# A two-layer hybrid block on one core: attention's side projections in three-matmul steps

## The chip, the cores and the metric

The kernel runs on one core of a Trainium2 chip. A core has TensorE (PE: matmuls and weight loads), VectorE (DVE), ScalarE (ACT), GpSimd (POOL) and SyncE (SP), which here only issues DMAs. The metric is the device time of one execution in microseconds. Each engine works through its own instructions in a fixed order and waits on semaphores for the others.

## The reference

A block of depth 2 on 512 tokens of width 1024, all in float32. Each layer normalises the input, projects it by one wide matrix, runs three branches on the parts (attention, retention, a gated convolution of 31 taps), mixes them by gates and adds a feed-forward part:

```python
for l in range(DEPTH):
    h = _rmsnorm(x, norm_mix[l])
    z = h @ w_in[l]
    (q_n, kc, vc, ks, vs, kw, vw, g_n, q_r, k_r, v_r, g_r, c_a, c_b, m_g) = _split_cols(z)
    o_nsa = _nsa(q_n, kc, vc, ks, vs, kw, vw, g_n, ...)
    o_ret = _retention(q_r, k_r, v_r, g_r, ret_gn[l])
    o_conv = _conv_module(c_a, c_b, conv_w[l], ...)
    proj = jnp.einsum('bsnc,ncd->bsnd', br, w_branch[l])
    gate = jax.nn.sigmoid(m_g.astype(jnp.float32)).reshape(B, S, N_BRANCH, D_MODEL)
    merged = jnp.sum(gate * proj, axis=2).astype(x.dtype)
    x = x + merged @ w_out[l]
    h2 = _rmsnorm(x, norm_mlp[l])
    x = x + jnp.square(jax.nn.relu(h2 @ w_ff1[l])) @ w_ff2[l]
```

The attention has 8 heads in 2 groups. Each head attends to 31 compressed blocks, to selected blocks and to a window, with a bias by distance; three gates weigh the three results. With 512 tokens the selection takes every block, and the window reaches over all.

## The kernel before, in words

Activations lie transposed: channels on the partitions, 512 tokens along the free dimension. Every operand of a large matmul is split into a high and a low part, and `proj` adds up three matmuls for each of the 8 channel blocks (high by high, high by low, low by high): 24 matmuls of 512 columns for one 128-wide output, 12 where the input has 4 blocks. A weight block is loaded by SP into one of three `wr` buffers (L139), rounded by ScalarE into `wh` (L145), and its remainder is taken by GpSimd in two halves into `wl` (L148), three buffers each; in the feed-forward part VectorE takes the remainder (L150).

A layer runs in these stages. The norm. Retention over 4 heads, with the inputs of the convolution made between them; the convolution's 124 taps are VectorE instructions of 512 columns (L338), put in small numbers behind other VectorE instructions by `conv_taps_behind` (`T_ROT`, `T_SCORE`, `T_KEYS`). The keys: two compressions (`compress`), one set of side work (`F_KEYS`), two key projections (L556 to L563), the values for all 4 token blocks in 4 PSUM tiles (`mm` three times and `av`, L568 to L576), and 6 taps behind them. Attention: 4 pairs of heads, each pair one query projection (`query`, L643) and 4 blocks (2 heads by 2 branches). A block has 4 slots by token block: scores into `sc` (L707), bias and maximum on VectorE (L712), exponential on ScalarE (L714), the scale by gate and sum (`gate_over`, L627 to L629), and then for each slot a scaled copy (L719), 1 to 4 transposes into `tp` (L722), a rounded copy by ScalarE (L727) and the remainder by VectorE (L728); the block ends with 8 matmuls by the values into `av`. The rest of the taps is spread over the first 52 of 64 slots, then the convolution's norm runs in parts (`conv_norm`). Then the mix of the branches, the output projection and the feed-forward part.

Beside the attention runs side work, the list `pending`: 8 mixes of retention's result (a gate of 24 matmuls and a branch projection of 12) and 16 gates for the other branches, stored to DRAM until they are needed. One goes ahead of the keys. `fill` writes out whole units: 19 are dealt over the 16 blocks, each traced at the end of its block and allowed on TensorE once that block's first score was issued; 4 are kept for the end:

```python
u = 4 * j + k
with tc.issue_after(marks[u].ins):
    fill(paced * (u + 1) // 16 - paced * u // 16)
```

The order on each engine comes from a planner. It walks the program with times of its own, takes the ready instruction that was traced first, and so may put later instructions ahead of earlier ones that it holds to be waiting; `tc.issue_after(i)` adds that what is traced inside stands behind `i` on `i`'s engine. Tiles of one tag share `bufs` buffers, in SBUF pools that open and close by stage: the pool `att` of attention takes memory that `keys` gave back, and its tiles wait for the last use there. `bias` and `tq` lie in `att`. The bias tables are written to DRAM in the first layer's keys stage (`late_setup`, L264 to L266) and read by L661. PSUM has 3 buffers for `mm`, 2 for `sc`, 2 for `tp`, 1 for `av`.

Of the kernel before, what the change touches and what calls it, by code (L numbers as in the profile page):

```python
# [14 lines left out]
OP = mybir.AluOpType  # L15
AX = mybir.AxisListType

P = 128
# [3 lines left out]
KC = D // P  # L22
# [44 lines left out]
def block_kernel(ctx: ExitStack, tc: tile.TileContext, a, out):  # L67
# [9 lines left out]

    T_ROT, T_SCORE, T_KEYS, T_SLOTS = 1, 2, 3, 52


    AHEAD, F_KEYS, HELD = 16, 1, 4

# [74 lines left out]
    def proj(o, w, x, nk=KC):  # L157

        h, l = w
        for k in range(nk):  # L160
            xh, xl = x[k]
            mm(o, h[:, k, :], xh, k == 0, False)
            mm(o, h[:, k, :], xl, False, False)
            last = mm(o, l[:, k, :], xh, False, k == nk - 1)
        return last

# [103 lines left out]
    for l in range(DEPTH):  # L270
# [117 lines left out]
        for h in range(4):  # L388
# [45 lines left out]
            hh, ll = bo(), bo()  # L434
            split(hh, ll, ot)
            RO.append((hh, ll))
# [5 lines left out]
        gated = set()  # L442

        def gate(n, m):
            pg = ps("mm")
            proj(pg, wblock(w_f[FB_MG + n * KC + m]), X)
            t = tl(base, "g", 3)
            nc.vector.tensor_mul(t, pg, rs)
            nc.scalar.activation(t, t, AF.Tanh, scale=0.5)
            return t  # L450

        def gate_ahead(n, m):
            dma(gdram[n * KC + m], gate(n, m))
            gated.add((n, m))

        def mix(n, o, m):
            if (n, m) in gated:
                t = tl(base, "g", 3)
                dma(t, gdram[n * KC + m])
            else:  # L460
                t = gate(n, m)
            po = ps("mm")
            proj(po, wblock(a["w_b"][l, n, m], 4), o, 4)
            nc.vector.scalar_tensor_tensor(t, t, 1.0, po, op0=OP.add, op1=OP.mult)
            if n == 1:
                dma(mdram[m], t)
            else:
                nc.vector.tensor_add(merged[m], merged[m], t)

        pending = [lambda m=m: mix(1, RO, m) for m in range(KC)]  # L470
        pending += [lambda k=k: gate_ahead(2 * (k // KC), k % KC) for k in range(AHEAD)]
        paced = len(pending) - F_KEYS - HELD

        def fill(n):
            for _ in range(min(n, len(pending))):
                pending.pop(0)()

# [6 lines left out]

        def compress(fb, w1, w2, pe_at, is_k):
            pz = ps("mm")
# [28 lines left out]
            if is_k:  # L515
                hid = small((P, 62))
                nc.vector.scalar_tensor_tensor(hid, s, 1.0, ph[:, :62], op0=OP.add, op1=OP.mult)
                w2t = small((P, P))
                dma(w2t[:, 0:64], w2)
                dma(w2t[:, 64:128], w2)  # L520
# [12 lines left out]
            w2t = small((P, 64))  # L533
            dma(w2t, w2)
            pv = ps("tp")
# [10 lines left out]

        kcb = compress(FB_KC, a["cmp_w1_k"][l], a["cmp_w2_k"][l], 32, True)
        vcb = compress(FB_VC, a["cmp_w1_v"][l], a["cmp_w2_v"][l], 48, False)

        fill(F_KEYS)  # L550
        KHH, KLL = {}, {}
        for br, fb in ((0, FB_KS), (1, FB_KW)):
# [4 lines left out]
            for g in range(2):  # L557
# [4 lines left out]
                for half in (nat, oth):  # L562
                    low = nc.vector.tensor_sub(KLL[br, g][half], t[nat], f(KHH[br, g][nat]))  # L563
            conv_taps_behind(low, T_KEYS)
        G = tl(mix_pool, "G", 1, (P, NB, 24))
        V = []
        pz = [ps(tag) for tag in ("mm", "mm", "mm", "av")]
        proj_tok([p[:, :280] for p in pz], [(a["w_v"][l][:, k0:k0 + nk], nk) for k0, nk in ((0, 3), (3, 3), (6, 2))], 280, X)  # L568
        for i in range(NB):
# [6 lines left out]
            V.append(v)  # L576
        conv_taps_behind(low, 2 * T_KEYS)
        phase.close()
# [63 lines left out]

        def query(j):  # L643
            w = wblock(w_f[FB_Q + j])
            pq = ps("mm")
            proj(pq, w, X)
            tq = tl(ap, "tq", 2)
            nc.vector.scalar_tensor_tensor(tq, pq, -0.125, rs, op0=OP.mult, op1=OP.mult)
            return tq

        def attention_pair(j, tq, more):
            QS, bias = [], []
            for g in range(2):
                nat, oth = halves(g)
                q = tl(ap, "QS", 3, (P, T), FR)
                nc.scalar.activation(q[nat], tq[nat], AF.Copy)
                nc.vector.tensor_sub(q[oth], tq[nat], f(q[nat]))
                QS.append(q)
                t = tl(ap, "bias", 3)
                src = fd[g * HPG + j]  # L660
                dma(t, bass.AP(tensor=src.tensor, offset=src.offset + P - 1, ap=[[FLEN - 1, P], [1, T]]))  # L661
                bias.append(t)
# [32 lines left out]
            for g in range(2):  # L695
# [4 lines left out]
                for br in range(2):  # L700
# [3 lines left out]
                    for i in range(NB):  # L704
                        n = P * (i + 1)
                        sc = ps("sc")
                        m0 = mm(sc[:, :n], QS[g][:, i * P:(i + 1) * P], KHH[br, g][:, :n], True, False)  # L707
                        if i == 0:
                            marks.append(m0)
                        mm(sc[:, :n], QS[g][:, i * P:(i + 1) * P], KLL[br, g][:, :n], False, True)  # L710
# [3 lines left out]
                        nc.scalar.activation(s, s, AF.Exp, scale=-1.0, bias=mx[:, i:i + 1], accum_out=den[:, i:i + 1])  # L714
                        cols.append(s)
                    c = gate_over(den, h, 1 + br)
                    ph, pl = tl(ap, "pt", 4, (P, 1280), FR), tl(ap, "pt", 4, (P, 1280), FR)
                    for i in range(NB):
                        nc.scalar.activation(cols[i], cols[i], AF.Copy, scale=c[:, i:i + 1])  # L719
                        pt = ps("tp")  # L720
                        for k in range(i + 1):
                            nc.tensor.transpose(pt[:, k * P:(k + 1) * P], cols[i][:, k * P:(k + 1) * P], ident)  # L722
                        for (vh, ks), (vl, _) in zip(pt_views(ph, i), pt_views(pl, i)):
# [17 lines left out]

        ON, marks, tqs = [], [], [query(0)]
        late_taps = len(todo)

        def more(j, k):

            if k == 0 and j + 1 < HPG:
                tqs.append(query(j + 1))
# [139 lines left out]
```

## Time and profile before

| what | value |
|---|---|
| time, median of 3 runs | 1802.95 us (1802.86 to 1805.15) |
| the profiled execution, its own time | 1804.74 us |
| its span, first to last instruction | 1803.0 us |
| mean granted TensorE clock | 0.984 |
| TensorE busy | 1757.3 us, 97% |
| weight loads busy | 1473.8 us, 82% |
| VectorE busy | 1104.4 us, 61% |
| ScalarE busy | 774.9 us, 43% |
| GpSimd busy | 500.6 us, 28% |
| DMA, mean | 109 GB/s |

The span is the time from the first to the last instruction; the execution's own time has a little around it. A matmul's end is modelled and matmuls overlap, so a busy TensorE need not be at its peak; the granted clock says at what share of its full rate it was allowed to run. Weight loads run beside matmuls. Idle time of an engine that sets no end costs nothing.

### The profile page before, as it was taken

How to read it: one execution, taken by the hardware profiler on the slowest of the kernel's cores; microseconds unless marked ns; L12 is line 12 of the kernel's file. 1: busy time of each engine (PE TensorE's matmuls, PEld its weight loads, DVE VectorE, ACT ScalarE, POOL GpSimd, SP SyncE). 2: the span in 40 equal slices, each digit the busy share in tenths (PEclk: the TensorE clock that was granted, in tenths of full speed). 3: DMA queues.
4: the chain of work that ended last, by engine and by line, in shares of the span. 5: the costliest groups of instructions: out<-in, count | busy, mean ns of one | idle time of the engine just before them, and what ended most of it. 6: DMA issues, size and time to landing. Idle time of an engine off the chain costs nothing.

```text
span 1803.0 us, 23260 instructions
## 1 busy us (share of the span) xinstructions
PE 1757.3 (97%) x8592; PEld 1473.8 (82%) x8592; DVE 1104.4 (61%) x1979; ACT 774.9 (43%) x1421; POOL 500.6 (28%) x420
## 2 busy tenths in 40 slices
PE   8899899989999999999999999999899999999997
PEld 7788788868888888888898888888688888888886
DVE  6976978887554344434459778878857443434344
ACT  4433466766343232323434344667553341323241
POOL 4454444323471000000255543343137500000000
PEclk9999999989999999999999999999899999999998
DMA  4222623221753323333422232332147323332321
GB/s 167 87 88 61 203 94 122 96 71 65 233 169 96 101 96 93 95 96 102 135 94 89 87 127 83 98 131 90 41 161 227 119 94 94 93 94 94 105 85 68
DMA packets 70802, 195.82 MB, mean 109 GB/s; under 512 B 8945, under 2 KB 9329, under 8 KB 70689
## 3 DMA queue, kind: packets, MB, share of 16 engines
q1 hardware_dynamic: 70688, 194.34, 33.6%
q8 instruction: 68, 1.11, 0.3%
q14 instruction: 46, 0.37, 0.1%
HBM read 177.51 MB, written 19.42 MB: 109 GB/s over the span
## 4 chain that ended last, share of the span: by engine, by line
PE 67%; issue 20%; DVE 10%; ACT 2%; DMA 1%; SPq 0%; POOLq 0%; POOL 0%; DVEq 0%; ACTq 0%
PE mm L109 58%; PE sc L109 3%; DVE yc L338 3%; PE av L109 3%; PE tp L722 2%; PE tp L109 1%; DVE XP L500 1%; DVE kv L563 1%; DVE qk L386 1%; ACT s L719 0%; DVE pt L728 0%; ACT wh L145 0%; DVE rr L364 0%; PE tp L190 0%; DVE s L712 0%
## 5 line engine op out<-in xcount | busy, mean ns | idle before, releaser
L109 PE MATMUL mm<-X,wh 128*128 128x512 f32 x2432 | 777.4, 396 | 12.2 <-ACT X L214 6.1
L148 POOL TENSOR_TENSOR wl<-wr,wh 128x512 fp32r<-128x512 f32 (+2 forms) x344 | 436.2, 1290 | 563.2 <-ACT wh L145 540.6
L145 ACT ACTIVATE wh<-wr 128x1024 fp32r<-128x1024 f32 (+2 forms) x301 | 296.9, 987 | 681.9 <-PE mm L109 554.5
L109 PEld LDWEIGHTS mm<-X,wh 128*128 128x128 f32 x2432 | 455.3, 189 | 103.1 <-ACT X L214 6.3
L109 PE MATMUL mm<-X,wl 128*128 128x512 f32 x1216 | 479.5, 394 | 0.4 <-DVE wl L150 0.4
L109 PEld LDWEIGHTS mm<-X,wl 128*128 128x128 f32 x1216 | 230.2, 189 | 46.5 <-DVE wl L150 0.9
L338 DVE SCALAR_TENSOR_TENSOR yc<-u,ccol,yc 128x512 f32<-128x512 f32 x240 | 214.2, 894 | 1.7
L150 DVE TENSOR_TENSOR wl<-wr,wh 128x1024 fp32r<-128x1024 f32 x129 | 158.1, 1225 | 38.4 <-ACT wh L145 38.4
L109 PE MATMUL mm<-fa,wh 128*128 128x512 f32 x512 | 160.2, 395 | 0.0
L109 PE MATMUL mm<-bo,wh 128*128 128x512 f32 x512 | 160.0, 391 | 0.0
L805 DVE SCALAR_TENSOR_TENSOR t<-mm,rs 128x512 f32<-128x512 f32 x64 | 43.9, 691 | 161.5 <-PE mm L109 155.9
L227 POOL TENSOR_TENSOR t<-t,t 128x512 f32<-128x512 f32 x18 | 27.4, 1523 | 333.7 <-DVE wl L150 310.7
L206 POOL TENSOR_TENSOR n<-n,mhalf 128x4 f32<-128x4 f32 x15 | 16.5, 1101 | 372.3 <-DVE n L204 372.3
L109 PE MATMUL mm<-kv,wh 128*128 128x512 f32 x384 | 119.5, 389 | 0.0
L109 PEld LDWEIGHTS mm<-fa,wh 128*128 128x128 f32 x512 | 96.1, 188 | 23.2
L109 PEld LDWEIGHTS mm<-bo,wh 128*128 128x128 f32 x512 | 96.0, 188 | 19.7
L109 PE MATMUL mm<-fa,wl 128*128 128x512 f32 x256 | 100.5, 395 | 0.0
L109 PE MATMUL mm<-bo,wl 128*128 128x512 f32 x256 | 100.2, 392 | 0.0
L714 ACT ACTIVATE s<-s,n 128x128 f32<-128x128 f32 (+3 forms) x128 | 71.4, 559 | 46.9 <-DVE n L712 46.3
L109 PE MATMUL mm<-wh,X 128*128 128x256 f32 (+1 forms) x480 | 90.1, 286 | 0.0
L728 DVE TENSOR_TENSOR pt<-tp,pt 128x128 fp32r<-128x128 f32 (+1 forms) x192 | 70.0, 372 | 32.7 <-ACT pt L727 32.4
L816 DVE TENSOR_TENSOR yc<-yc,mm 128x512 f32<-128x512 f32 x32 | 22.0, 687 | 105.6 <-PE mm L109 105.6
(219 smaller groups left out, 2463.9 us busy)
## 6 DMA issues: line engine op xcount, KB each, us to landing
wr<-in_w_dram SPq DMA_DIRECT2D x128, 512.0 KB, 3.5
wr<-in_w_f_dram SPq DMA_DIRECT2D x87, 512.0 KB, 3.3
wr<-in_w_b_dram SPq DMA_DIRECT2D x48, 256.0 KB, 2.7
wr<-in_w_t_dram SPq DMA_DIRECT2D x16, 512.0 KB, 3.4
gd<-g SPq DMA_DIRECT2D x32, 256.0 KB, 2.0
g<-gd SPq DMA_DIRECT2D x32, 256.0 KB, 2.8
wr<-in_w_o_dram SPq DMA_DIRECT2D x16, 512.0 KB, 3.6
md<-g SPq DMA_DIRECT2D x16, 256.0 KB, 2.9
```

The lines of the kernel that those rows point to most:

```text
L109: return nc.tensor.matmul(o, l, r, start=start, stop=stop)
L145: nc.scalar.activation(h, t, AF.Copy)
L148: nc.gpsimd.tensor_sub(l[:, k], t[:, k], f(h[:, k]))
L150: nc.vector.tensor_sub(l, t, f(h))
L227: (nc.vector if c == KC - 1 or first_time else nc.gpsimd).tensor_add(s, s, acc)
L338: nc.vector.scalar_tensor_tensor(yc[c], x, w, yc[c], op0=OP.mult, op1=OP.add)
L386: nc.vector.tensor_sub(QLr[h][half], pt[nat], f(QHr[h][nat]))
L714: nc.scalar.activation(s, s, AF.Exp, scale=-1.0, bias=mx[:, i:i + 1], accum_out=den[:, i:i + 1])
L722: nc.tensor.transpose(pt[:, k * P:(k + 1) * P], cols[i][:, k * P:(k + 1) * P], ident)
L728: low = nc.vector.tensor_sub(vl, src, f(vh))
L805: nc.vector.scalar_tensor_tensor(t, pf, 0.0, rs, op0=OP.max, op1=OP.mult)
L816: nc.vector.tensor_add(xT[m], xT[m], pf)
```

## The change

The side work becomes generators. `proj_steps` yields after each three matmuls, and mixes and gates are written in such steps. A function `step(n)` runs the next n steps: 24 behind the first score of the first block, 5 behind the last score of each block of the last pair, and the rest, but for 16 that are left to the end, dealt evenly over the 64 slots, each behind the slot's last transpose. The weight block of a unit is asked for when its first step is taken. The bias tiles move to the layer's pool. The first query is projected ahead of the values, into a tile of the layer's pool. The second weights of the compressions are loaded at the start of the keys stage. The 6 taps behind the values are gone, 2 taps are added behind each retention head. `gate_ahead` is unpacked in the same way as the mix below; lines that only follow are left out.

```diff
-    T_ROT, T_SCORE, T_KEYS, T_SLOTS = 1, 2, 3, 52
-    AHEAD, F_KEYS, HELD = 16, 1, 4
+    T_ROT, T_SCORE, T_HEAD, T_KEYS, T_SLOTS = 1, 2, 2, 3, 52
+    AHEAD, F_KEYS, RAMP, HELD, LAST = 16, 1, 24, 5, 16
...
+    def proj_steps(o, w, x, nk=KC):
+
         h, l = w
         for k in range(nk):
             xh, xl = x[k]
             mm(o, h[:, k, :], xh, k == 0, False)
             mm(o, h[:, k, :], xl, False, False)
-            last = mm(o, l[:, k, :], xh, False, k == nk - 1)
-        return last
+            mm(o, l[:, k, :], xh, False, k == nk - 1)
+            yield
...
-            split(hh, ll, ot)
+            conv_taps_behind(split(hh, ll, ot), T_HEAD)
...
         def gate(n, m):
+            w = wblock(w_f[FB_MG + n * KC + m])
             pg = ps("mm")
-            proj(pg, wblock(w_f[FB_MG + n * KC + m]), X)
+            yield from proj_steps(pg, w, X)
...
-        pending = [lambda m=m: mix(1, RO, m) for m in range(KC)]
-        pending += [lambda k=k: gate_ahead(2 * (k // KC), k % KC) for k in range(AHEAD)]
-        paced = len(pending) - F_KEYS - HELD
+        pending = [(12, mix_steps(1, RO, m)) for m in range(KC)]
+        pending += [(8, gate_ahead(2 * (k // KC), k % KC)) for k in range(AHEAD)]
...
+        w2k, w2v = small((P, P)), small((P, 64))
+        for half in (slice(0, 64), slice(64, 128)):
+            dma(w2k[:, half], a["cmp_w2_k"][l])
+        dma(w2v, a["cmp_w2_v"][l])
...
+        def query(j, pool):
+            w = wblock(w_f[FB_Q + j])
+            pq = ps("mm")
+            proj(pq, w, X)
+            tq = tl(pool, "tq", 2 if j else 1)
+            nc.vector.scalar_tensor_tensor(tq, pq, -0.125, rs, op0=OP.mult, op1=OP.mult)
+            return tq
+
+        tqs = [query(0, mix_pool)]
         G = tl(mix_pool, "G", 1, (P, NB, 24))
...
-        conv_taps_behind(low, 2 * T_KEYS)
         phase.close()
...
-                t = tl(ap, "bias", 3)
+                t = tl(mix_pool, "bias", 3)
...
-                        m0 = mm(sc[:, :n], QS[g][:, i * P:(i + 1) * P], KHH[br, g][:, :n], True, False)
-                        if i == 0:
-                            marks.append(m0)
+                        scored = mm(sc[:, :n], QS[g][:, i * P:(i + 1) * P], KHH[br, g][:, :n], True, False)
+                        if j == g == br == i == 0:
+                            with tc.issue_after(scored.ins):
+                                step(RAMP)
...
+                    if j == HPG - 1:
+                        with tc.issue_after(scored.ins):
+                            step(HELD)
                     c = gate_over(den, h, 1 + br)
...
+                        with tc.issue_after(turned.ins):
+                            step(paced * (slot + 1) // 64 - paced * slot // 64)
...
+        def step(n):
+            for _ in range(n):
+                next(beside)
+
+        paced = sum(n for n, _ in pending) - RAMP - 4 * HELD - LAST
+        beside = itertools.chain(*(steps for _, steps in pending))
...
-            u = 4 * j + k
-            with tc.issue_after(marks[u].ins):
-                fill(paced * (u + 1) // 16 - paced * u // 16)
...
-        with tc.issue_after(marks[-1].ins):
-            fill(len(pending))
+        for _ in beside:
+            pass
```

`turned` is the slot's last transpose.

## Rows read from the trace of the kernel before

**Rows 1.** The page: span, and busy us, share of the span and instructions by engine.

```profile
span 1803.0 us, 23260 instructions
...
PE 1757.3 (97%) x8592; PEld 1473.8 (82%) x8592; DVE 1104.4 (61%) x1979; ACT 774.9 (43%) x1421; POOL 500.6 (28%) x420
```

**Rows 2.** The page: TensorE's granted clock in 40 slices, in tenths of full speed.

```profile
PEclk9999999989999999999999999999899999999998
```

**Rows 3.** Windows: stretch, length, busy of PE, PEld, DVE, ACT, POOL; clock, DMA, GB/s.

```profile
100.00:178.00 78.00, 78.00 (x426) 67.63 (x425) 52.38 (x83) 28.52 (x47) 37.42 (x31) 1.00 0.23 73
...
200.00:212.00 12.00, 7.31 (x22) 5.60 (x21) 11.96 (x18) 2.73 (x8) 4.86 (x4) 0.72 0.82 258
225.00:374.00 149.00, 148.59 (x765) 125.38 (x764) 119.77 (x328) 101.30 (x252) 58.40 (x49) 1.00 0.32 105
...
382.00:412.00 30.00, 22.98 (x104) 16.95 (x103) 25.93 (x73) 18.17 (x54) 2.64 (x2) 0.77 0.08 27
412.00:465.00 53.00, 53.00 (x262) 44.66 (x261) 32.78 (x68) 32.28 (x68) 17.37 (x15) 1.00 0.36 119
500.00:545.00 45.00, 45.00 (x200) 37.10 (x199) 24.80 (x28) 19.96 (x27) 33.96 (x25) 1.00 0.51 168
...
1085.00:1096.00 11.00, 8.92 (x47) 8.70 (x47) 10.71 (x19) 4.09 (x10) 3.19 (x3) 0.69 0.37 126
...
1264.00:1296.00 32.00, 25.25 (x112) 19.02 (x111) 27.65 (x78) 19.28 (x57) 2.63 (x2) 0.73 0.08 29
```

**Rows 4.** Groups by line, TensorE, 225 to 374 us: count, busy us, mean ns, idle.

```profile
L109 PE MATMUL mm<-X,wh 128*128 128x512 f32 x254 | 84.1, 401 | 0.0
L109 PE MATMUL mm<-X,wl 128*128 128x512 f32 x127 | 50.4, 397 | 0.0
...
L109 PE MATMUL mm<-bo,wh 128*128 128x512 f32 x56 | 17.7, 395 | 0.0
L722 PE MATMUL tp<-ident,s 128*128 128x128 f32 x99 | 17.2, 274 | 0.0
...
L109 PE MATMUL mm<-bo,wl 128*128 128x512 f32 x28 | 11.2, 402 | 0.0
```

**Rows 5.** Waits, 382 to 412 us: who waited for whom, us, times, longest.

```profile
PE av L109 <- ACT pt L727: 2.3, 4, 0.7
...
PE tp L722 <- DVE pt L728: 1.9, 2, 1.5
```

**Rows 6.** Timeline of POOL, 375 to 425 us: start, us, instruction, idle before and releaser.

```profile
382.21 2.64 POOL L148 TENSOR_TENSOR wl<-wr,wh 128x512 fp32r<-128x512 f32 x2 [5.03 <-PE tp L722]
```

**Rows 7.** Timeline of TensorE around 205 and 412 us.

```profile
205.10 1.22 PE L109 MATMUL mm<-X,wh 128*128 128x512 f32 x2 [4.69 <-ACT G L575]
...
412.31 0.71 PE L109 MATMUL mm<-X,wh 128*128 128x512 f32 x2
```

**Rows 8.** Groups by line and shape, TensorE, 382 to 412 us.

```profile
L722 PE MATMUL tp<-ident,s 128*128 128x128 f32 x40 | 9.1, 345 | 1.9 <-DVE pt L728 1.9
```

**Rows 9.** Groups by line, VectorE, 178 to 223 us: the convolution's taps.

```profile
L338 DVE SCALAR_TENSOR_TENSOR yc<-u,ccol,yc 128x512 f32<-128x512 f32 x23 | 21.2, 930 | 0.5
```

**Rows 10.** Timeline of VectorE around 220 us.

```profile
220.69 0.69 DVE L648 SCALAR_TENSOR_TENSOR tq<-mm,rs 128x512 f32<-128x512 f32 x1
```

**Rows 11.** Timeline of SP's DMA queue, 196 to 221 us.

```profile
196.41 5.12 SPq L266 DMA_DIRECT2D fd<-f  x8
...
220.69 0.33 SPq L661 DMA_DIRECT2D bias<-fd  x1
```

**Rows 12.** Groups by line, whole span: the softmax's steps.

```profile
L714 ACT ACTIVATE s<-s,n 128x128 f32<-128x128 f32 (+3 forms) x128 | 71.4, 559 | 46.9 <-DVE n L712 46.3
...
L719 ACT ACTIVATE s<-s,n 128x128 f32<-128x128 f32 (+3 forms) x128 | 61.9, 554 | 11.2 <-DVE n L629 11.1
...
L712 DVE CUSTOM_DVE_ANT_0 s<-sc,bias 128x128 f32<-128x128 f32 (+3 forms) x128 | 59.8, 483 | 13.5 <-PE sc L109 13.3
...
L627 DVE TENSOR_SCALAR n<-n 128x4 f32<-128x4 f32 x48 | 20.6, 444 | 9.9 <-ACT s L714 9.4
```

More of the change, by code (lines that the diff above doesn't have):

```diff
@@ L1 @@
+import itertools
 import math
@@ L157, in proj @@
     def proj(o, w, x, nk=KC):
+        for _ in proj_steps(o, w, x, nk):
+            pass
+    def proj_steps(o, w, x, nk=KC):
         h, l = w
@@ L452, in gate_ahead, with mix_steps @@
         def gate_ahead(n, m):
-            dma(gdram[n * KC + m], gate(n, m))
+            t = yield from gate(n, m)
+            dma(gdram[n * KC + m], t)
             gated.add((n, m))
-        def mix(n, o, m):
+        def mix_steps(n, o, m):
             if (n, m) in gated:
@@ L460, in mix @@
             else:
-                t = gate(n, m)
+                t = yield from gate(n, m)
+            w = wblock(a["w_b"][l, n, m], 4)
             po = ps("mm")
-            proj(po, wblock(a["w_b"][l, n, m], 4), o, 4)
+            yield from proj_steps(po, w, o, 4)
             nc.vector.scalar_tensor_tensor(t, t, 1.0, po, op0=OP.add, op1=OP.mult)
@@ L468, in mix @@
                 nc.vector.tensor_add(merged[m], merged[m], t)
-        pending = [lambda m=m: mix(1, RO, m) for m in range(KC)]
-        pending += [lambda k=k: gate_ahead(2 * (k // KC), k % KC) for k in range(AHEAD)]
-        paced = len(pending) - F_KEYS - HELD
+        def mix(n, o, m):
+            for _ in mix_steps(n, o, m):
+                pass
+        pending = [(12, mix_steps(1, RO, m)) for m in range(KC)]
+        pending += [(8, gate_ahead(2 * (k // KC), k % KC)) for k in range(AHEAD)]
         def fill(n):
             for _ in range(min(n, len(pending))):
-                pending.pop(0)()
+                for _ in pending.pop(0)[1]:
+                    pass
         phase.close()
@@ L532, in compress @@
                                                ph[:, :62].rearrange("p (g n) -> p g n", g=2), op0=OP.add, op1=OP.mult)
-            w2t = small((P, 64))
-            dma(w2t, w2)
             pv = ps("tp")
@@ L545, in compress @@
             return vc
-        kcb = compress(FB_KC, a["cmp_w1_k"][l], a["cmp_w2_k"][l], 32, True)
-        vcb = compress(FB_VC, a["cmp_w1_v"][l], a["cmp_w2_v"][l], 48, False)
+        kcb = compress(FB_KC, a["cmp_w1_k"][l], w2k, 32, True)
+        vcb = compress(FB_VC, a["cmp_w1_v"][l], w2v, 48, False)
         fill(F_KEYS)
@@ L641, in pt_views @@
             return r
[L643 to L649, printed above, removed]
         def attention_pair(j, tq, more):
@@ L721, in attention_pair @@
                         for k in range(i + 1):
-                            nc.tensor.transpose(pt[:, k * P:(k + 1) * P], cols[i][:, k * P:(k + 1) * P], ident)
+                            turned = nc.tensor.transpose(pt[:, k * P:(k + 1) * P], cols[i][:, k * P:(k + 1) * P], ident)
                         for (vh, ks), (vl, _) in zip(pt_views(ph, i), pt_views(pl, i)):
@@ L740, in attention_pair @@
             return oj
-        ON, marks, tqs = [], [], [query(0)]
+        ON = []
         late_taps = len(todo)
+        def step(n):
[3 more added lines that the diff above has]
+        beside = itertools.chain(*(steps for _, steps in pending))
         def more(j, k):
             if k == 0 and j + 1 < HPG:
-                tqs.append(query(j + 1))
+                tqs.append(query(j + 1, ap))
             if not todo:
                 next(normed, None)
-            u = 4 * j + k
-            with tc.issue_after(marks[u].ins):
-                fill(paced * (u + 1) // 16 - paced * u // 16)
         for j in range(HPG):
@@ L759, in block_kernel @@
             pass
-        with tc.issue_after(marks[-1].ins):
-            fill(len(pending))
+        for _ in beside:
+            pass
         phase.close()
```

5 lines of the change are left out of this document (1 added, 4 removed).

## The prediction

> **What bounds the kernel now.** I read the busy shares first: TensorE works 97% of the span, weight loads 82%, VectorE 61% [rows 1]. So time can only come from stretches where TensorE waits or runs at its lower clock. The 40 slices of granted clock show where: it falls under nine tenths at slices 9 and 29, about 360 and 1262 us in, and at the end [rows 2]. The table by stretch then says how much. The feed-forward stretch runs 200 matmuls of 512 columns in 45.00 us, 0.225 us each, at clock 1.00; attention from 225 to 374 us is as dense (148.59 of 149.00 us busy). But 382 to 412 us has 104 matmuls in 30 us at clock 0.77 (a mix of its levels 2.4 and 1.2 GHz), and its twin in the second layer, 1264 to 1296 us, 112 in 32 us at 0.73. 200 to 212 us has 22 in 12 us, 1085 to 1096 us 47 in 11 us [rows 3].
>
> What the dents cost I count in matmuls. In 225 to 374 us, 254 + 127 + 56 + 28 = 465 of the 765 are 512-column projections [rows 4]; at 0.225 they take 104.6 us, so attention's own 300 take 44.4 us, 0.148 each. By that price 104 need 15.4 us, and 30 - 15.4 = 14.6 us are lost; in the twin 32 - 112 x 0.148 = 15.4 us. In 200 to 212 us, mostly projections, 12 - 22 x 0.225 = 7.0 us are lost; in 1085 to 1096 us 11 - 47 x 0.148 = 4.0 us. Together 41.0 us can be had: 30.0 in the last pair of heads, 11.0 ahead of attention.
>
> Why the last pair stalls: no projection runs in 382 to 412 us, only attention's chain (transposes wait for VectorE's low parts, A x V for ScalarE's copies [rows 5]). Yet a gate's weights were split by 382.21 + 2.64 = 384.85 us [rows 6], and its first matmul ran at 412.31 [rows 7]. Work was there, behind attention in TensorE's order. The 53 us after it then hold what was missing [rows 3].
>
> Here the Trainium skill weighs the stretch differently ("Perfetto Trace Analysis", section "Identifying the Most-Contended Engine"): matmul busy time misleads, judge TensorE by the share of weight loads. That gives 30 x (1 - 16.95/30 / 0.824) = 9.4 us and 32 x (1 - 19.02/32 / 0.824) = 8.9 us, 0.824 being the feed-forward's 37.10/45 [rows 3]. By it the last pair would give 18.3 us and not 30.0, and my sum would come out near 1787 us. No run here tells yet which is right; I keep the count, since it rests on the matmuls that the stretch must do, whatever the clock.
>
> **Side projections in steps.** The same matmuls remain. A mix is 12 steps, a gate 8; 8 x 12 + 16 x 8 = 224 steps, less 12 for the mix ahead of the keys = 212. Of these 24 go behind the first score, 5 behind each of the last pair's four score groups, 16 to the end; 152 are dealt over 64 slots, 2.375 steps or 7.1 matmuls, 1.60 us, behind each slot's last transpose. Before, 19 units went behind 16 blocks, 19 - 14 = 5 of them in the last pair, and 4 were held: 9 gates, 72 steps; it now has 38 + 20 + 16 = 74. The amount is the same; the place is new. The stretch 382 to 412 us holds 40 transposes [rows 8], 16 slots: 16 x 1.60 = 25.7 us of projections now go there, more than the 14.6 us lost. I take 2 us per layer as remaining: gain 30.0 - 4.0 = 26.0 us (0 if the steps don't land there, 30.0 at most). The end stays covered: 16 steps x 0.675 = 10.8 us behind the last transposes.
>
> What is late next is VectorE. In 225 to 374 us it was busy 119.77 us [rows 3] for 99 transposes [rows 4], 39.6 slots: 3.0 us each, with the side evictions of a denser mix in it. TensorE's new slot is 1.60 + (44.4/39.6 =) 1.12 + 0.25 for the queries (72 x 0.225 over 64) = 2.97 us. The two are nearly level; the 24 steps at the start, 16 us, let VectorE run ahead. No row shows attention at that pace with projections: the nearest, 225 to 374 us, stalls 0.4 us, the bare chain of 382 to 412 us idles 7.0 us on 16 slots. Over 64 slots that is 0.2 to 28 us per layer; I take 3, near the first row, since side work stands between the transposes: +6.0 us.
>
> **First query ahead of the values.** After the values TensorE waits 4.69 us for their PSUM tiles, until ScalarE's G [rows 7], which stands behind VectorE's backlog. The query's 24 matmuls (5.4 us) now run before the values, so these end 5.4 us later, and VectorE loses the 6 taps behind the values, 6 x 0.93 = 5.6 us [rows 9]; the query's eviction, which ran at 220.69 us [rows 10], is no longer behind them. Both exceed the wait. Against it: the third PSUM tile of the values now waits for the query's eviction on a full VectorE, and the query no longer fills the time behind the values; the second one, the two compressions and the first 24 steps must. Of the 11.0 us I take 9.0 as won (bounds -3 to 11).
>
> **Bias tiles, small weights.** Both are DMAs on SP. The first bias load was issued at 220.69 us, after the keys' memory came free; in its own pool it can go as soon as the table is written (from 196.41 us) [rows 11]. In the first layer it then waits for that write, whose issue alone takes 5.12 us, and the next weight loads stand behind it in SP's queue: 0 to 5 us, I take +1.0. The small weights, three loads, move to the stage's start, past weight loads; they pass before the values' blocks and gain nothing that a row shows: 0, at most 1 us either way.
>
> **Two taps behind each retention head.** 8 per layer, into 100 to 178 us mostly, where VectorE is busy 52.38 of 78 us and TensorE all of it [rows 3]: hidden. If the first head's two delay TensorE they cost 1.9 us per layer; I take +0.5 in all.
>
> **Sum.** -26.0 - 9.0 + 6.0 + 1.0 + 0.5 = -27.5 us. The span of 1803.0 us becomes 1775.5, the profiled execution of 1804.74 us 1777.2. The median of the runs, 1802.95 us, lies 1.8 us below that execution, so I forecast 1775 us.
>
> **Rivals.**
> 1. *The steps fill the dents* (forecast): 1758 to 1783 us, chance 0.57. All 41.0 won and no new stall is 1762 us; 8 us worse than the sum is 1783.
> 2. *VectorE becomes the second bound.* 0.1 us of stall at each of 128 slots is 12.8 us where I have 6.0, and the half of a dent that it leaves takes 7 more: 1783 to 1799 us, say 1789. For it: the level 3.0 and 2.97 us. Against it: fewer side evictions per slot, and VectorE busy only 25.93 of 30 us where the chain ran fastest [rows 3]. Chance 0.20.
> 3. *Slower: the next scores lose their head start.* A block's scores now stand in the program behind the steps of the block before, whose issue hangs on its transposes. If TensorE takes them only then, each block bares one softmax latency: 0.483 + 0.559 + 0.444 + 0.554 = 2.04 us [rows 12]. The last pair has its 5 steps there; the other 12 blocks of each layer have none: 24 x 2.04 = 49 us, against 27.5 won: 1824 us. It decides from 27.5/24 = 1.15 us per block. For it: scores are the only cover inside a block between steps. Against it: they depend on nothing in the block before, and TensorE's order was made so that they ran early. 1807 to 1850 us, chance 0.15.
> 4. *It doesn't do what it says*: the dents aren't a matter of order, and the steps sit behind the same chain. The gate that waited 27 us with its weights split speaks against it. 1799.5 to 1806.5 us, chance 0.08.
>
> **Chances.** Within 0.2% (3.6 us, about what a measurement here can tell from no change) is rival 4, 0.08; slower is rival 3, 0.15; faster are 1 and 2, 0.77. The range 1758 to 1804 us leaves out rival 3 and the top of 4, little below. The forecast's own range is 1758 to 1783.
>
> **What would show it.** Right: in the last pair of both layers projections between the transposes, granted clock 1.00 there, and the dense stretch behind them shorter by some 40 us; no wait of about 4.7 us on G behind the values; bias loads ahead of the keys' end. Wrong: TensorE waiting on VectorE's low parts in many slots (rival 2), waits of 1 to 2 us ahead of each block's first transpose (rival 3), or a dent of 30 us still there (rival 4). The count of matmuls is wrong if the dents close and less than 20 us comes back.

## The result: slower, with the dent it aimed at gone

The changed kernel takes 1823.99 us (median of 4 runs, 1823.3 to 1824.17); the kernel before took 1802.9 in the same rounds. The ratio is 1.0114, 95% interval 1.0097 to 1.0132: 21 us slower, where the forecast of 1775 us was 28 us faster. The sign was wrong.

The page of the changed kernel, busy us by engine and the granted clock in 40 slices:

```profile
span 1821.5 us, 23249 instructions
...
PE 1762.5 (97%) x8592; PEld 1473.1 (81%) x8592; DVE 1109.1 (61%) x1979; ACT 772.1 (42%) x1421; POOL 509.1 (28%) x420
...
PEclk9999899999999999999999998999999999999998
```

Against [rows 1] the span is 18.5 us longer with the same matmuls and the same 97%. A share of busy time hides such a change: a matmul at the lower clock is busy too. Against [rows 2] the low slices moved: slices 9 and 29 are whole again, 5 and 25 are low, the start of attention in either layer. The windows tell more (stretch, length, busy of PE, PEld, DVE, ACT, POOL; clock, DMA, GB/s):

```profile
185.00:200.00 15.00, 12.29 (x64) 10.07 (x63) 14.89 (x21) 7.25 (x12) 6.41 (x5) 0.89 0.50 181
215.00:225.00 10.00, 7.82 (x24) 6.13 (x24) 6.94 (x31) 1.89 (x5) 0.41 (x2) 0.66 0.41 148
225.00:248.00 23.00, 20.98 (x91) 16.33 (x90) 8.89 (x32) 13.08 (x33) 7.94 (x8) 0.93 0.36 115
...
380.00:425.00 45.00, 44.29 (x236) 37.36 (x235) 33.33 (x87) 28.46 (x70) 17.08 (x12) 1.00 0.31 106
425.00:440.00 15.00, 10.51 (x41) 8.40 (x40) 8.61 (x18) 7.85 (x17) 3.51 (x2) 0.77 0.09 35
440.00:470.00 30.00, 30.00 (x152) 25.18 (x151) 20.13 (x46) 18.95 (x41) 9.35 (x9) 1.00 0.31 93
```

The last pair, 104 matmuls in 30 us at clock 0.77 before [rows 3], is now dense: 236 in 45 us at 1.00. Two stretches that were whole are not: behind attention's first score (225 to 248 us) and at the last softmax (425 to 440; so called here and below, it is that of the last block but one, the last block's own is covered). Ahead of attention (185 to 225), where the kernel before had its loss at 200 to 212, time is now lost in two places. At the 0.197 us per matmul of 440 to 470 us, the last has lost 15 - 41 x 0.197 = 6.9 us. The timeline there (start, us, instruction, idle before and releaser):

```profile
428.15 0.62 PE L111 MATMUL sc<-kv,QS 128*128 128x128 f32 x4
433.25 0.48 PE L743 MATMUL tp<-ident,s 128*128 128x128 f32 x1 [4.49 <-ACT s L740]
433.38 1.20 PE L111 MATMUL mm<-X,wh 128*128 128x512 f32 x2
434.38 0.63 PE L111 MATMUL mm<-X,wl 128*128 128x512 f32 x1
434.81 1.05 PE L111 MATMUL mm<-X,wh 128*128 128x512 f32 x2
...
438.59 0.39 PE L111 MATMUL mm<-X,wl 128*128 128x512 f32 x1
438.82 0.49 PE L743 MATMUL tp<-ident,s 128*128 128x128 f32 x3
```

The wait costs 4.49 us and then more: behind it two matmuls take 0.85 to 1.0 us from start to start, against 0.46 when the clock is whole (granted 0.77 over the 15 us, so partly at 1.2 GHz). This wait is paid about one and a half times.

I counted all stretches this way, each matmul at the start-to-start time of its shape where nothing waits (0.23 us for 512 columns). The counts are estimates: matmuls of 128 columns start 0.03 to 0.11 us apart, and by the choice of their price the last pair of the kernel before comes out at 16 to 22 us. The difference of the two spans doesn't hang on it, since both run the same matmuls. Us lost, where the two kernels differ most:

| stretch | before | after |
|---|---|---|
| first layer, values and first score | 8.0 | 5.5 + 4.9 |
| scores behind the ramp | none | 5.5 |
| last pair / last softmax | 17.1 | 0 / 6.8 |
| second layer, retention's heads | none | 4.7 |
| ahead of attention | 4.7 | 10.3 |
| scores behind the ramp | none | 4.3 |
| last pair / last softmax | 17.8 | 0 / 7.5 |
| four short ones inside attention | none | 12.9 |
| sum | 47.6 | 62.4 |

That is 14.8 of the 18.5 us. In the first 20 us the matmuls fall behind by 0.8 more; they are late before SP issues the first small weights (12.87 us), and why isn't shown. The rest is small differences elsewhere, in both directions. From the second layer's first merge to the end both kernels take 454 us.

### The profile page after: what moved, and what is told of

The parts are those of the page before. It is cut to its first block, busy times and chain, and to the rows that moved or that the text cites. A ratio compares the mean times of both kernels' runs of the same rounds, so it can differ in the third digit from the quotient of the medians.

```text
span 1821.5 us, 23249 instructions
## 1 busy us (share of the span) xinstructions
PE 1762.5 (97%) x8592; PEld 1473.1 (81%) x8592; DVE 1109.1 (61%) x1979; ACT 772.1 (42%) x1421; POOL 509.1 (28%) x420
## 4 chain that ended last, share of the span: by engine, by line
PE 58%; issue 21%; DVE 18%; ACT 2%; DMA 0%; SPq 0%; POOLq 0%; POOL 0%; DVEq 0%; ACTq 0%
PE mm L111 51%; DVE yc L345 5%; PE sc L111 2%; PE av L111 2%; PE tp L743 1%; DVE pt L749 1%; PE tp L111 1%; DVE s L730 1%; DVE kv L579 1%; ACT s L732 1%; DVE QS L674 1%; ACT s L740 1%; DVE n L652 1%; DVE qk L393 1%; DVE pr L115 1%
## 5 line engine op out<-in xcount | busy, mean ns | idle before, releaser
L150 POOL TENSOR_TENSOR wl<-wr,wh 128x512 fp32r<-128x512 f32 (+2 forms) x344 | 444.2, 1313 | 549.2 <-ACT wh L147 523.4
L147 ACT ACTIVATE wh<-wr 128x1024 fp32r<-128x1024 f32 (+1 forms) x301 | 296.3, 986 | 690.4 <-PE mm L111 538.0
L345 DVE SCALAR_TENSOR_TENSOR yc<-u,ccol,yc 128x512 f32<-128x512 f32 x240 | 223.7, 934 | 1.9
L749 DVE TENSOR_TENSOR pt<-tp,pt 128x256 fp32r<-128x256 f32 (+1 forms) x192 | 71.2, 374 | 59.3 <-ACT pt L748 58.8
L111 PE MATMUL mm<-wh,X 128*128 128x256 f32 (+1 forms) x480 | 95.0, 297 | 3.8 <-ACT wh L147 2.1
L748 ACT ACTIVATE pt<-tp 128x256 fp32r<-128x256 f32 (+1 forms) x192 | 62.9, 338 | 59.1 <-PE tp L743 38.7
```

The lines of the kernel that those rows point to most:

```text
L111: return nc.tensor.matmul(o, l, r, start=start, stop=stop)
L147: nc.scalar.activation(h, t, AF.Copy)
L150: nc.gpsimd.tensor_sub(l[:, k], t[:, k], f(h[:, k]))
L345: nc.vector.scalar_tensor_tensor(yc[c], x, w, yc[c], op0=OP.mult, op1=OP.add)
L748: nc.scalar.activation(vh, src, AF.Copy)
L749: low = nc.vector.tensor_sub(vl, src, f(vh))
```

## Experiments

Two theories. A, order: the edits took away work that covered waits, so each new loss can be closed by putting a cover back. B, VectorE: its work has no slack in attention, so a loss closed in one place opens in another. Each edit also lets the planner order all engines anew, so what a run shows is the edit together with the order that it brought. The kernel before ran beside each group, 1804.5 to 1805.1 us; "dent" is a stretch with such a loss.

**The halves apart.** The kernel before with the steps alone, and with everything but the steps (whole units as before):

```diff
 steps_alone: as the change, but
-        tqs = [query(0, mix_pool)]            # ahead of the values
+        ON, tqs = [], [query(0, ap)]          # behind them, as before; also the bias tiles,
...                                            # the small weights and the taps as before
 rest_alone: as the change, but
-                        with tc.issue_after(turned.ins): step(...)
+            with tc.issue_after(marks[u].ins): fill(...)   # as before
```

> The steps alone in the kernel before: bias tiles, first query, small weights and taps as they were. Theory A (the steps close the last pair's dent of 30 us but open new ones: 24 steps ahead of the first block's scores, 5.2 and 4.5 us; pair starts without side work, 4.8 and 5.5 us; the last block's softmax, 6.8 and 7.8 us): about 1805 to 1815 us, slower than before, and all these dents still in the trace. Theory B (the steps gain as forecast, and the other parts spoil it in the keys stage): 1775 to 1785 us.

> Everything but the steps: whole units behind each block's first score as before, 4 held, with bias tiles in the layer's pool, first query ahead of the values, small weights early, two taps behind each retention head and none behind the values. Theory A: the keys stage loses a few us per layer and one retention head 5 us, 1805 to 1816 us, with the dent of 30 us in the last pair as before. Theory B: it loses what the steps would have won, 1835 to 1850 us.

1818.3 us (ratio 1.0079, 1.0064 to 1.0094) and 1819.8 (1.0083, 1.0067 to 1.0100), both 3 to 4 us above the top of theory A's ranges. Each half alone loses 14 to 15 us, both together 21. rest_alone keeps the last pair's dents. The steps close them and lose it elsewhere, about 6 us at 215 to 225, 12 to 13 at 1095 to 1120, some 7 at each last softmax.

**No ramp; the query behind the values again.**

```diff
 ramp0:      RAMP, HELD, LAST = 24, 5, 16  ->  0, 5, 16
 query_back: tqs = [query(0, mix_pool)]  ->  ON, tqs = [], [query(0, ap)] behind the values
```

> The changed kernel with RAMP = 0: the 24 steps are dealt over the 64 slots (2.75 each) and none stands behind the first score. Theory A (they stand ahead of the first block's other scores and starve VectorE for 14 us): attention starts its transposes 10 us or more earlier, 1805 to 1815 us. Rival (they are the only cover for the first softmax): the dent at the first block grows, 1824 us or more.

> The changed kernel with the first query behind the values again, its tile in attention's pool. Theory A (the query no longer covers the time behind the values, and its split waits for the keys' memory anyway): the dents at 189 to 200 and 214 to 225 us shrink, 1814 to 1820 us. Rival (the query ahead is neutral or helps): 1824 us or more.

ramp0 is 1817.7 us (1.0076, 1.0060 to 1.0092), 6 below the change and between the two expectations: without the ramp the first scores are bare (some 12 us lost at 215 to 235, 16 to 20 at 1090 to 1130). query_back is 1832.3 (1.0155, 1.0140 to 1.0170), where theory A had the direction wrong: TensorE waits 5.8 us for G again. So the query ahead of the values was good for some 7 us, near the 9.0 of the forecast.

**The second query's cover.** In the kernel before this query is traced ahead of the units, and its 24 matmuls run before the first score. With the steps, the ramp is traced inside the first block; its weight blocks go into the three weight buffers first (in steps_alone SP issues two blocks of `w_b`, which only mixes use, at 190.69 and 202.41 us), and TensorE meets the first score bare.

```diff
 s_q1 = steps_alone with
-        ON, tqs = [], [query(0, ap)]
+        ON, tqs = [], [query(0, ap), query(1, ap)]
...
-            if k == 0 and j + 1 < HPG:
+            if k == 0 and 0 < j < HPG - 1:
```

> The steps alone, and the second query of the first pair traced ahead of the first block, as the kernel before ran it. Theory A (order): in the steps the weight blocks of the 24-step ramp stand ahead of this query's, so nothing covers the start of attention; with the query back in front, the losses at 215 to 225 us (6.4 us) and at 1095 to 1120 us (15.0 us) of the steps alone shrink to half or less, which is 8 to 14 us: 1804 to 1811 us against 1818.3. Theory B (VectorE cannot follow the denser mix, wherever the work stands): the losses only move, 1815 to 1820 us.

1803.96 us (0.9998, 0.9988 to 1.0007): 14.3 below steps_alone, at the fast end of theory A's expectation. By the count 13.9 of the 14.3 come back at the two starts of attention. Whether the buffers or TensorE's order held the query back, this run doesn't separate: it moves both. Windows, first of steps_alone, then of s_q1:

```profile
212.00:226.00 14.00, 11.44 (x59) 9.94 (x58) 12.61 (x29) 2.86 (x6) 3.35 (x3) 0.77 0.26 78
1095.00:1120.00 25.00, 20.02 (x86) 17.38 (x85) 23.33 (x49) 6.49 (x17) 8.19 (x7) 0.67 0.24 76
```

```profile
212.00:226.00 14.00, 13.59 (x83) 11.92 (x82) 13.46 (x32) 3.84 (x7) 3.95 (x5) 1.00 0.33 98
1088.00:1113.00 25.00, 24.78 (x120) 21.86 (x121) 24.17 (x45) 8.08 (x19) 10.50 (x9) 0.86 0.26 87
382.00:415.00 33.00, 33.00 (x174) 27.74 (x172) 23.08 (x56) 20.32 (x49) 10.79 (x8) 1.00 0.31 110
415.00:435.00 20.00, 15.52 (x74) 12.92 (x73) 11.56 (x26) 11.30 (x25) 6.03 (x4) 0.83 0.18 66
```

In the first layer the start is whole, the last pair too (33.00 of 33 us), and yet the time is that of before: by the count 35 us are won in the last pairs and nearly as many lost, about 7 at each last softmax, 4.5 and 5.0 at the scores behind the ramp, the rest in waits of below 2 us each.

**Taps behind the retention heads.**

```diff
 thead0 = the change with
-            conv_taps_behind(split(hh, ll, ot), T_HEAD)
+            split(hh, ll, ot)
```

> The changed kernel without the two taps behind each retention head; they go back to the tap list that attention works off. Theory A: they cost the second layer's start of attention 4.7 us (the loss at 1025 to 1035 us) and add nothing elsewhere: 1818 to 1821 us against 1824. Rival: they relieve VectorE in attention, and without them its backlog grows by 16 taps of 0.93 us, 15 us over both layers, part of it seen: 1824 to 1832 us.

1812.5 us (1.0043, 1.0028 to 1.0058), 11.5 below the change, more than twice what theory A gave them. The timelines of the changed kernel around 1030 us, VectorE and then TensorE, show why:

```profile
1027.50 1.22 DVE L115 TENSOR_TENSOR pr<-rt,pr 128x512 fp32r<-128x512 f32 x1
1028.64 1.77 DVE L345 SCALAR_TENSOR_TENSOR yc<-u,ccol,yc 128x512 f32<-128x512 f32 x1
1030.33 1.61 DVE L115 TENSOR_TENSOR pr<-rt,pr 128x384 fp32r<-128x384 f32 x1
```

```profile
1032.00 0.67 PE L111 MATMUL av<-pr,v 128*128 128x384 f32 x2 [1.86 <-DVE pr L115]
```

A tap stands between two steps of the next head's decayed scores, and the head waits for it. The backlog also reaches the values, by way of ScalarE, whose copies wait for VectorE and stand ahead of a weight copy (TensorE waits 2.15 us for it, L147): 64 matmuls in 185 to 200 us at clock 0.89 in the change; in thead0:

```profile
185.00:200.00 15.00, 14.55 (x98) 12.52 (x97) 13.58 (x18) 7.67 (x14) 6.87 (x5) 1.00 0.68 229
1010.00:1030.00 20.00, 20.00 (x95) 16.82 (x94) 18.13 (x26) 7.70 (x15) 11.63 (x10) 1.00 0.27 85
```

**Both mended.** thead0 with the second query ahead of the first block:

```diff
 a_q1t0 = thead0 with
         ON = []
+        tqs.append(query(1, ap))
...
-            if k == 0 and j + 1 < HPG:
+            if k == 0 and 0 < j < HPG - 1:
```

> The changed kernel with two places mended: the second query traced ahead of the first block, and no taps behind the retention heads. Theory A (order): each removes a cost of its own, 14.3 us for the query's cover (measured on the steps alone) and 11.5 us for the taps (measured on the changed kernel), so that 1824 comes to 1796 to 1802 us, just below the kernel before. Rival: both relieve the same start of the second layer's attention and don't add, 1808 to 1813 us.

1802.1 us (0.9986, 0.9976 to 0.9995): 10.4 below thead0, at the edge of theory A's range. The two account for the whole loss and no more. But here the cover closes only the first layer's start (some 4 us by the count). The second layer's start loses over 9 us in both thead0 and a_q1t0: TensorE waits for the eviction of the first query, now ahead of the values, a cost that the forecast had named. In a_q1t0:

```profile
1081.00 0.83 PE L111 MATMUL mm<-wh,X 128*128 128x280 f32 x2 [3.19 <-DVE tq L587]
```

Most of the rest comes back inside the second layer's attention; why isn't shown.

**Other places for the steps.** s_all: ramp behind the first block's last score, 14 steps behind the last block's scores (its expectation says the last three blocks; the edit gives the other three of the last pair 5 each), 7 at the end. s_both_tail: the steps dealt over 128 places, 8 behind the first block's scores, 14 behind the last one's, 10 at the end. s_mix: the same with 14 between the halves of the first score and 16 at the end. a_mix: s_mix's dealing on a_q1t0.

```diff
 s_mix = s_q1 with
-    RAMP, HELD, LAST = 24, 5, 16
+    RAMP, HELD, TAIL, LAST = 14, 3, 14, 16
...
+                        with tc.issue_after(scored.ins): deal()   # behind each score
...
-                            step(paced * (slot + 1) // 64 - paced * slot // 64)
+                            deal()                                # and each slot
```

> The steps alone with three places mended: the second query ahead of the first block, the 24-step ramp behind the last score of the first block and not between the halves of its first one, and 14 steps behind the scores of the last three blocks, 7 at the end. Theory A (order): the start, the ramp's dents (240 to 250 and 1135 to 1145 us, 10 us) and those of the last softmax (430 to 445 and 1320 to 1335 us, 13 us) mostly close: 1785 to 1800 us, below the kernel before. Theory B (VectorE): 1810 to 1820 us, with the losses spread over the slots.

> As the one before, but the steps dealt over 128 places, one behind each score and one behind each slot's transposes, so that no five to eight scores stand in a row without a step, and 10 at the end. Theory A (order): what is left of idle time between scores goes too, 1778 to 1795 us, and 3 to 8 us below the kernel before it in this list. Theory B (VectorE): no better than it, 1810 to 1820 us.

> The steps alone with the second query ahead of the first block, 14 steps between the halves of the first score, the rest dealt over 128 places (behind each score and each slot's transposes), 3 behind each score group of the last pair, 14 behind the last group, 16 at the end. Theory A (order): against 1804.4 of its neighbour with 8 and 10 steps at these two places, the losses at 220 to 235 and 1105 to 1120 us (15.7 us) halve and those ahead of the merges (460 to 470, 1345 to 1355 us, 7.8 us) go: 1788 to 1797 us. Theory B (VectorE): the losses reappear elsewhere, 1800 to 1806 us.

> The same dealing on the changed kernel without the taps behind the retention heads, so with the first query ahead of the values, the bias tiles in the layer's pool and the small weights early. Theory A: 6 to 10 us better than the same dealing without those parts, 1780 to 1791 us, the fastest of all. Theory B: 1796 to 1806 us.

s_all is 1830.8 us (1.0149, 1.0132 to 1.0166), against both theories: the ramp between the halves of the first score had covered the compressed softmax (TensorE now waits 3.54 us there), and 7 steps at the end don't reach over the last heads' splits (4.91 us). s_both_tail is 1804.4 (0.9995, 0.9986 to 1.0005), between the theories. s_mix is 1801.2 (0.9977, 0.9968 to 0.9986), the fastest of the kernels that do all the work, some 4 us below the kernel before. Its last softmax is covered, but small waits on VectorE are spread over the slots, as theory B has it:

```profile
382.00:412.00 30.00, 28.37 (x149) 23.76 (x148) 24.87 (x66) 19.21 (x50) 9.87 (x7) 1.00 0.23 80
415.00:435.00 20.00, 20.00 (x108) 16.89 (x108) 13.28 (x40) 13.88 (x36) 5.78 (x5) 1.00 0.30 104
```

a_mix, with the change's other parts added, is 1808.1 (1.0015, 1.0005 to 1.0024): slower than s_mix and than either theory had it. Why is not settled; it loses 6.3 us at 1305 to 1320 us, and TensorE waits 2.9 us for VectorE's L653 at 415 to 435 us.

**VectorE's load.** The taps inside attention left out, but for the first of each chunk; the kernel so leaves out part of the convolution:

```diff
 s_q1_notap = s_q1 with, from the start of attention on,
                 n -= 1
+                if k and skip:
+                    continue
```

> The steps alone with the second query ahead, and without the convolution's taps that run inside attention (all but the first of each chunk; 59 instructions of 915 ns in the first layer, 54 of VectorE's 186 busy us there). This leaves out part of the convolution; only its time counts. Theory B (VectorE's load is the second bound): most of the losses inside attention, some 30 us, go, 1770 to 1785 us. Theory A (order: the losses lie at 240 to 250 and 420 to 435 us, where no tap runs): 1797 to 1803 us.

1793.7 us (0.9933, 0.9916 to 0.9949): 10.2 below s_q1, between the theories. 54 and 58 us of VectorE's work in the two layers are gone and only 5 us are won in each. The 4.5 us at the last softmax stay, the small waits go.

**The convolution's norm.** At the last softmax, VectorE of the changed kernel:

```profile
422.07 0.16 DVE L618 TENSOR_SCALAR n<-mm 128x4 f32<-128x4 f32 x1 [0.83 <-PE mm L111]
422.15 0.28 DVE L730 CUSTOM_DVE_ANT_0 s<-sc,bias 128x128 f32<-128x128 f32 x1
...
423.86 2.48 DVE L622 TENSOR_TENSOR yc<-yc,mm 128x512 f32<-128x512 f32 x4 [1.07 <-PE mm L197]
426.25 0.67 DVE L762 TENSOR_TENSOR on<-t,av 64x512 f32<-64x512 f32 x1
426.85 0.54 DVE L730 CUSTOM_DVE_ANT_0 s<-sc,bias 128x384 f32<-128x384 f32 x1
...
427.94 0.68 DVE L626 TENSOR_TENSOR u<-u,u 128x512 f32<-128x512 f32 x1
428.54 0.68 DVE L457 TENSOR_TENSOR g<-mm,rs 128x512 f32<-128x512 f32 x1
429.14 0.68 DVE L626 TENSOR_TENSOR u<-u,u 128x512 f32<-128x512 f32 x1
429.83 1.14 DVE L652 TENSOR_SCALAR n<-n 128x4 f32<-128x4 f32 x1
430.89 0.68 DVE L626 TENSOR_TENSOR u<-u,u 128x512 f32<-128x512 f32 x1
431.49 0.16 DVE L653 RECIPROCAL n<-n 128x4 f32<-128x4 f32 x1
431.69 1.02 DVE L654 SCALAR_TENSOR_TENSOR n<-G,n 128x4 f32<-128x4 f32 x1
```

VectorE meets this block's scores (L730) between parts of the norm. The first one left TensorE by 402.2 us and is taken at 422.15, behind a step of the norm (L618) that waits for TensorE's column sums. The last two ran on TensorE from 423.57 to 424.6 and are taken only from 426.85 on, behind the norm's four subtractions (L622). Later one of its sums (L626) stands between two of the softmax's three tiny steps (L652 to L654). So the norm was moved between the merges (a_norm), with the ramp divided as well (a_norm_ramp), in the kernel before too (b_norm), and forward, by working the taps off sooner:

```diff
 a_norm = a_q1t0, b_norm = the kernel before, with
-            if not todo:
-                next(normed, None)
...
             mix(0, OS, m)
+            next(normed, None)
 a_norm_ramp: RAMP 16, and step(1) behind each of the first eight scores
 a_t44, a_t36 = a_q1t0 with T_SLOTS 44, 36 for 52; a_t44_ramp with that ramp
```

> The changed kernel with the query's cover back and no taps at the retention heads, and the convolution's norm (the squares, sums and the normalising of four tiles on VectorE and ScalarE) moved out of the last blocks of attention, between the merges behind it. Theory A: the last block's first transpose waits 4.5 us in each layer because VectorE has this norm's work ahead of the softmax's small steps; with it gone the losses at 415 to 430 us (7.4 us) and 1300 to 1315 us (6.3 us) close, 1786 to 1793 us against 1802.1. Rival: the wait is the softmax's own latency with nothing to cover it, or the norm stalls the merges by as much: 1798 to 1804 us.

> As a_norm, with the ramp's 24 steps divided: 16 between the halves of the first score, one behind each of the first eight scores. Theory A: the losses of 4.0 and 5.1 us at 235 to 245 and 1120 to 1135 us, where eight scores stand in a row behind the ramp and wait 0.2 to 0.75 us each for VectorE's reductions, shrink by half or more: 4 to 8 us below a_norm. Theory B: VectorE sets this pace, the steps only move the wait, within 2 us of a_norm.

> The kernel before with only the convolution's norm moved in the same way: what that move is worth without the steps. Theory A: the last pair's loss is one of missing work between the transposes, the norm only lengthens it, 2 to 6 us of its 35 us go: 1799 to 1803 us. Rival: the norm was most of that loss, and the steps were never needed: below 1790 us.

> The changed kernel with the query's cover back and no taps at the retention heads (1802.1 us), and the taps dealt over the first 44 of the 64 slots in place of 52, so that the convolution's norm comes two blocks of four slots earlier, with attention's work still behind it. Theory A: the norm costs its 7 us only where nothing stands behind it; two blocks earlier the last softmax's losses (7.4 and 6.3 us) close and at most 2 us a layer come up elsewhere, 1789 to 1795 us. Theory B (VectorE): the taps come 18% denser and stall the slots before, the loss only moves, 1799 to 1808 us.

> As a_t44, with the ramp divided, 16 between the halves of the first score and one behind each of the first eight. Theory A: 1 to 4 us below a_t44 (this division gave 1.7 us with the norm moved away). Theory B: no difference, or worse.

> As a_t44 with 36 slots, the norm four blocks earlier and the taps 44% denser than at 52. Theory A: as a_t44 within 3 us, while VectorE still has room. Theory B (VectorE): slower than a_t44 by 3 us or more.

a_norm: 1814.6 us (1.0058, 1.0043 to 1.0073), a_norm_ramp 1812.9 (1.0048, 1.0033 to 1.0063). Attention's last matmul ends at 448.5 instead of 455.0 us (a_q1t0) and the loss at the last softmax is gone, in both layers: the norm did make it late. (TensorE's order around it changed as well.) But the norm's chain then stalls the merges: from the first of them to the feed-forward's second product it is 145.3 instead of 133.1 us, worse than either theory had it. Windows of a_norm:

```profile
410.00:430.00 20.00, 20.00 (x103) 16.82 (x102) 11.23 (x36) 13.93 (x36) 5.12 (x4) 1.00 0.28 92
455.00:485.00 30.00, 25.09 (x108) 20.45 (x107) 17.79 (x29) 8.09 (x14) 13.19 (x15) 0.89 0.52 170
```

b_norm: 1818.5 (1.0079, 1.0062 to 1.0096), slower where both theories had it faster, for the same reason behind attention. But it bears on the forecast's base. Without the norm the last pair of the kernel before runs like this, with no step in it; below the window are its projections there, and the first of them:

```profile
382.00:412.00 30.00, 26.04 (x126) 21.65 (x127) 20.44 (x55) 19.22 (x50) 6.59 (x5) 0.94 0.22 79
...
L109 PE MATMUL mm<-X,wh 128*128 128x512 f32 x46 | 15.0, 408 | 0.0
L109 PE MATMUL mm<-X,wl 128*128 128x512 f32 x22 | 8.7, 395 | 0.0
...
384.64 0.68 PE L109 MATMUL mm<-X,wh 128*128 128x512 f32 x2
```

26.04 us busy and 126 matmuls, against 22.98 and 104 [rows 3], and by the count some 7 us lost and not 17.1. This isn't VectorE's relief: 68 of the 126 matmuls are projections of whole units, where the kernel before ran none until 412.31 us [rows 7]. On VectorE the norm had little to do with that dent; in the kernel before its first instructions come at the dent's end:

```profile
408.46 0.68 DVE L589 TENSOR_TENSOR u<-yc,yc 128x512 f32<-128x512 f32 x1
...
409.40 0.68 DVE L590 TENSOR_TENSOR u<-u,u 128x512 f32<-128x512 f32 x1
```

So the dent was one of order, as the forecast had it: with the norm out of the way, TensorE's order let whole units in some 26 us earlier. Why the norm kept them out (the planner's choice, or the `mm` tiles that its sums use too) isn't shown.

a_t44: 1809.2 (1.0021, 1.0012 to 1.0031), just above theory B's range; a_t44_ramp 1804.6 (0.9991, 0.9979 to 1.0003), more than theory A gave the divided ramp; a_t36 1827.7 (1.0127, 1.0108 to 1.0147). Two blocks earlier the norm stalls TensorE all the same, 6.8 us at 390 to 405 and 8.5 at 1275 to 1295, and with the taps 44% denser it costs 25.6 us over a_q1t0. For earlier taps theory B holds: in these orders VectorE has no room for them inside attention.

## Why the prediction was wrong

**Right.** The order kept work out of the last pair, and the steps brought it in: its dents went by 34.9 us in the count (17.1 + 17.8), where I took 26.0 of 30.0. The price used there stands up as well: s_both_tail does 92 projections and 66 of attention's matmuls in 382 to 412 us, TensorE busy throughout, so attention's take (30 - 92 x 0.225)/66 = 0.141 us, where I had 0.148:

```profile
382.00:412.00 30.00, 30.00 (x158) 25.49 (x157) 25.84 (x68) 21.90 (x53) 9.68 (x8) 1.00 0.29 103
```

The estimate worked out from the Trainium skill's measure by weight loads ("Perfetto Trace Analysis", section "Identifying the Most-Contended Engine"), 9.4 us for that stretch, was too low here: 104 x 0.141 leaves 15.3 us. The base of 41.0 us and its reading, "Work was there, behind attention in TensorE's order", hold: in b_norm whole units run in that stretch. The first query was worth about 7 us (ratio 1.0155 with it behind the values, 1.0114 ahead), where I had 9.0.

**Wrong: "the second one, the two compressions and the first 24 steps must" fill the time before the first score.** I named the second query as the cover and did not follow its weights. The 24 steps are traced before it and take the weight buffers ahead of it. Measured: 14.3 us (steps_alone to s_q1), 10.4 (thead0 to a_q1t0, only some 4 of it at a start). Of the 11.0 us ahead of attention I had kept back 2.0, for this and for the values' third tile together.

**Wrong: "Two taps behind each retention head ... hidden", +0.5.** They cost 11.5 us. The ground was a mean, VectorE 52.38 of 78 us busy [rows 3]; the place is a chain (L115 to the head's matmul) in which VectorE is the next to act, and a tap of up to 1.77 us goes in between.

**Mis-sized: "I take 2 us per layer as remaining".** At the last softmax 6.8 and 7.5 us are lost, 14.3 where I had 4.0. I looked only for work that TensorE lacked; what is late here is the softmax on VectorE, behind the convolution's norm (L618, L622; a_norm). The row I read as slack, VectorE "busy only 25.93 of 30 us", is 86%. Where the norm was moved, the loss came up in its new place (a_norm, a_t44).

**Mis-sized: body stalls, +6.0.** In the changed kernel 5.5 and 4.3 us are lost at the scores behind the ramp and 12.9 in four short stretches inside attention: 22.7 us. That "the 24 steps at the start, 16 us, let VectorE run ahead" was backwards: eight scores stand behind the ramp in TensorE's order, and VectorE is busy 8.89 of 23 us there, waiting for TensorE. The lower bound was a slip, too: 0.4 us over 39.6 slots is 0.7 us over 64, not 0.2; the sum doesn't use it.

**The rivals.** Rival 3 named 1824 us, but by 24 bare softmax latencies; the trace shows one long wait per layer (4.49 us, at the last block but one) and the losses of the other steps. Its number was a coincidence. Rival 2, VectorE as second bound, is much of what remains once the two omissions are mended (10.2 us go with the taps, and the last softmax waits for the norm): s_q1 and a_q1t0 come out at 1802 to 1804 us, above the top of its range.

**Left open.** Why the norm in the kernel before kept whole units out of the last pair, why the dealing of s_mix loses when the change's other parts join it (a_mix), and whether any order gets much below 1801 us without lightening VectorE.

## What to carry to other kernels

When work is re-traced in a scheduled kernel, follow what it overtakes in buffers and queues, weights first: what was a cover is one only while its operands arrive. Where a wait stays although work is there, look at the in-order queue of the engine that is waited for, and ask what stands ahead of the few small instructions that matter. When a run moves one piece and a stretch gets shorter, read what fills the stretch before the gain is put down to that piece. A mean share of an engine (52 of 78 us) says nothing of an instruction put between two links of a chain.

## What the runs showed of the hardware

A wait of 4.5 us cost about 7: in the changed kernel TensorE idled 4.49 us until 433.25 us; behind that the granted clock was 0.51 for 5.6 us, so nearly all of it at 1.2 GHz, and matmuls of 512 columns ran 0.43 to 0.5 us apart; from 438.6 us on it was 1.00 and they ran 0.23 us apart.

```profile
433.00:438.60 5.60, 5.35 (x15) 4.24 (x16) 0.72 (x2) 2.38 (x6) 0.00 (x0) 0.51 0.12 47
438.60:441.00 2.40, 2.40 (x14) 1.97 (x13) 0.72 (x2) 0.66 (x2) 0.00 (x0) 1.00 0.00 0
```

And a tap of one shape takes 729 to 1850 ns (median 748) over the 240 of the changed kernel: what is hidden by its median can be late by its maximum.
